# Two PSUM banks for projections and six shared, with new step delays and a new first stage, in a two-layer decoder trunk

## The chip, the core and the metric

The kernel runs on one core of one Trainium2 chip. The core has five engines with a queue of instructions each: TensorE (PE, matrix products), VectorE (DVE), ScalarE (ACT), GpSimd (POOL) and SyncE (SP, which here only issues DMA transfers). Each engine runs its queue in order; engines wait for one another through semaphores. The metric is the device time of one execution in microseconds (us).

## The reference

Everything is float32: 1024 tokens of width 1024, and two layers. Cut to what matters, one layer is:

```python
shift, scale, gate = split(silu(c) @ W_mod + b_mod)
h = rms_norm(x, gain_pre) * (1 + scale) + shift
p = h @ W_in                      # 1024 x 3088, split in three head groups
A = sliding_window_attention(...) # 8 heads, 2 kv heads, window 128
B = retention(...)                # 4 heads, chunks of 128
C = gated_linear_attention(...)   # "GLA": 4 heads, key width 32, chunks of 64
y = concat(A, B, C, each times silu(its gate path)) @ W_out
x = x + gate * rms_norm(y, gain_post)
```

B and C are normalised per head first, and C's decay is computed from the data.

## The kernel before

**Numbers in halves.** Each float32 matrix is split into a high and a low part of a shorter type. A product of two such matrices takes three passes (high by high, high by low, low by high). `project`, `project_T`, `project_2`, `accum` and `prod` emit them: mostly 24 matmuls of 128x512 for one tile of 128 tokens, into one PSUM bank. `mult` (L170) and `transp` (L185) emit every matmul and every transpose, so nearly all PE rows of the profile carry one of these two lines; the tile names tell them apart. `mm` stands for a bank of a projection or an output product, `aux` for a bank of everything else (transposes, scores, states), `arena` for weights.

**Weights.** A weight arrives by DMA in a stage tile `st` (five of these in use), is converted to its high part (ACT L154 or DVE L156, `arena<-st`) and its low part (DVE or POOL L504). These conversions stand in the same in-order queues as all other work of ACT, DVE and POOL, so one that waits for its DMA holds up what is queued behind it.

**PSUM.** There are eight banks of 128x512 float32. `mm()` rotates over `MMB` = 3 of them, `aux()` over the other five. A matmul into a bank waits until the readers of that bank's last content (the "eviction") are done.

**Order on PE.** The program keeps a clock `clk` of its own, to which each matmul adds its length. Work is cut into jobs, generators that emit some instructions and then `yield lat(key, l)`: a delay, after which the job may go on. The delay is a value of the table `L` for the key (a second one for layer 2, `key@1`), plus what the table `X` has for this very occurrence (`"gc2#7"` is the seventh call with key `gc2`). `pump()`, called between matmuls, resumes the jobs whose time has come. So these numbers decide between which matmuls of a projection a small step lands, and nothing else does on PE. Other engines are ordered by the framework's scheduler, which follows from it.

The jobs that matter below: `glaout` ends with two transposes into an `aux` bank, which ACT (L154) and DVE (L1115) then empty. `attnkv` transposes a key tile into an `aux` bank (ACT L988, DVE L989). `glacore` (key names `gc1` to `gc6`) works on a pair of tokens' tiles `p`: two transposes, and then for each of two halves 56 matmuls of 32 rows into four `aux` banks at once, which ACT L1269 and DVE L1270 empty (a "score burst").

**The first stage** (up to 46.6 us) has its order written out by hand: `ORDER_0` for the DMA issues (x0 to x3 parts of the input, w0 to w7 the eight 1 MB parts of `W_mod`, g a part of the first weights), `ORDER_1` for the steps. There S0 to S7 are the products with w0 to w7, C and L take up their results, M and N make the scaled halves of the input, P and Q the first projection's sums, T and U transposes of the input; z and y are fillers, matmuls of a constant whose result is not used. `GLO` says who makes the low halves of two of the first weights.

Of the kernel before, what the change touches and what calls it, by code (L numbers as in the profile page):

```python
# [26 lines left out]
AQ, AK, AV, AG = 0, 512, 640, 768  # L27
# [64 lines left out]
def trunk(ctx: ExitStack, tc: tile.TileContext, ins, cst, out):  # L92
# [40 lines left out]
    def aux(dt=F32):  # L133
        return ps.tile([P, 512], dt, tag="aux", name=nm("aux"), bufs=8 - MMB)

# [579 lines left out]
    def first_stage():  # L715
# [59 lines left out]
        pc = mm()  # L775
# [599 lines left out]
    def y_half(l, t, nh, mixt, ss, yg):  # L1375
        pm = mm()
        w0, w1 = used(l, f"o{2 * nh}"), used(l, f"o{2 * nh + 1}")
        accum(pm.rearrange("p (s n) -> p s n", s=2),
              lambda a, k: mixt[:, a, k, :], lambda b, k: both(w0[:, b, k, 0:256], w1[:, b, k, 0:256]))
        A.activation(yg, pm, AF.Square, accum_out=ss[:, nh:nh + 1])  # L1380
        V.tensor_tensor(yg, pm, modg[l][:, 512 * nh:512 * nh + 512], ALU.mult)

    def y_last(l, mixt, ss, yg):
        s3 = small(3)
        for u in range(2):
            pm = mm()[:, 0:256]
# [121 lines left out]
    def last_output(l, load_mix):  # L1508
# [24 lines left out]
        for p in range(PLAIN // 2):  # L1533
            x, ss, yg = [], [], []
            for t in (2 * p, 2 * p + 1):
                if t + 1 < PLAIN:
                    m[t + 1] = load_mix(l, t + 1)
                x.append(mm())
# [7 lines left out]
            for i, t in enumerate((2 * p, 2 * p + 1)):  # L1546
# [5 lines left out]
                y = mm()  # L1552
# [13 lines left out]
        for p in range(PLAIN // 2, NP_):  # L1566
# [9 lines left out]
            pm = mm()  # L1576
            prod(pm, cur.a[0], "W00")
            s1 = kept(pm)
            pm = mm()
# [4 lines left out]
            pm = mm()  # L1584
# [9 lines left out]
            pm = mm()  # L1594
# [5 lines left out]
            pm = mm()  # L1600
# [3 lines left out]
            if nxt:  # L1604
                nxt.late()
                pump()
                pm = mm()
                prod(pm, a22, "T4")
                summed(yg[o][0], pm, s1, ss[o][:, 0:1], 0)
                job(finish(l, o, ss[o][:, 0:2], yg[o]))  # L1610
                pump()
                continue
# [4 lines left out]
            pm = mm()  # L1617
# [3 lines left out]
            pm = mm()  # L1621
# [10 lines left out]
    def layer(l):  # L1632
# [3 lines left out]
        def do_gates(name, p):  # L1636
            w = used(l, name)
            for t in (2 * p, 2 * p + 1):
                pg = mm()
# [195 lines left out]
ORDER_0 = "g x1 x0 w0 g w1 x2 w2 g w3 w4 x3 w5 w6"  # L1835
ORDER_1 = (
# [4 lines left out]
)  # L1841
GLO = {'AG': (2, 3), 'AV': (1, 0, 2)}
B2, B1, BS, BST, MMB, SMB, BMOD = 10, 8, 11, 5, 3, 3, 3
# [39 lines left out]
}  # L1883
L = {"fx": 0.0, "fx@1": 3.19, "tt6": 10.91, "sw1": 2.36, "ld1": 1.66, "ld2": 1.76, "ld1@1": 0, "ld2@1": 0, "swW00": 5.37, "swT1": 0.43, "swW11": 1.72, "swW10": 6.42, "tt1": 15.2, "tt2": 5.14, "tt3": 7.18, "tt4": 1.84, "rq1": 17.87, "pf3@2": 0.45, "pf3@3": 0.47, "pf4@2": 4.68, "pf4@3": 9.7, "pf5": 0, "mod1": 12.02, "mod2": 2.2, "mod3": 8.51, "mod4": 8.65, "mod5": 4.17, "mod6": 9.91, "pre1": 11.53, "kv1": 4.21, "kv2": 9.26, "aq1": 6.02, "aq7": 6.16, "ag1": 4.54, "aq2": 2.75, "aq6": 6.87, "aq3": 11.06, "aq4": 6.77, "aq5": 4.05, "hn1": 8.92, "hn2": 7.95, "gz1": 18.33, "gz2": 13.43, "gl1": 9.02, "gd3": 17.03, "gc1": 0.98, "gc2": 6.16, "gc3": 1.97, "gc4": 0.1, "gc6": 0.8, "gc5": 1.4, "rc1": 3.56, "rc2": 2.88, "rc3": 7.08, "rc4": 5.77, "fin1": 8.81, "lay1": 0.0, "gc4@1": 0, "mod2@1": 3.98, "mod3@1": 12.43, "mod5@1": 4.3, "mod6@1": 5.5, "pre1@1": 7.09, "kv1@1": 5.87, "kv2@1": 2.64, "aq1@1": 4.85, "aq7@1": 5.14, "ag1@1": 2.87, "aq2@1": 1.05, "aq6@1": 6.78, "aq3@1": 8.64, "aq4@1": 5.47, "aq5@1": 5.83, "hn1@1": 8.28, "hn2@1": 1.35, "gz1@1": 15.9, "gz2@1": 11.94, "gl1@1": 3.26, "gd3@1": 15.44, "gc1@1": 0.0, "gc2@1": 2.01, "gc3@1": 0.83, "gc6@1": 1.61, "gc5@1": 0.72, "rc1@1": 4.88, "rc2@1": 2.79, "rc3@1": 5.12, "rc4@1": 1.23, "fin1@1": 6.41, "lay1@1": 12.76, "mod4@1": 5.36, "mod1@1": 6.02}
# [45 lines left out]
```

## Time and profile before

| what | value |
|---|---|
| three runs | 976.16, 977.75 and 978.88 us, median 977.75 |
| the profiled execution | 978.04 us, span of its trace 976.3 us |
| PE busy | 959.7 us, 98% of the span |
| DVE, ACT, POOL busy | 669.2, 411.0, 247.1 us |
| matmuls | 6296 records |
| DMA | 150.23 MB, mean 154 GB/s |

The profiled execution lies 0.3 us above the median. The span is what the trace covers; 1.7 us of the time lie around it. "PE busy" counts overlapping matmuls as one stretch, and a matmul that runs at half clock is as busy as one at full clock, so busy time alone does not show whether PE worked at its speed; the granted clock (PEclk) has to be read beside it.

### The profile page before, as it was taken

To read this page: it belongs to the slowest core of one execution; us is meant where nothing else is said; L and a number is where in the kernel's file an instruction comes from. 1 tells how busy PE (TensorE), PEld (TensorE's weight loads), DVE (VectorE), ACT (ScalarE), POOL (GpSimd) and SP (SyncE) were. 2 spreads that over 40 slices of the span, in tenths; PEclk is the share of its full clock that TensorE was granted. 3 is DMA by queue.
4 is the path that set the end of the run, shared out by engine and by line. 5 is a ranking of instruction groups with operands and counts; after the bars stand their busy time and mean duration, and the time that the engine had idled before them with its cause. 6 is when DMAs were issued, how large, how long until landed. Compare 5 with 4: busy or idle time off the path is not lost.

```text
span 976.3 us, 17846 instructions
## 1 busy us (share of the span) xinstructions
PE 959.7 (98%) x6296; PEld 787.1 (81%) x6296; DVE 669.2 (69%) x1585; ACT 411.0 (42%) x1147; POOL 247.1 (25%) x310
## 2 busy tenths in 40 slices
PE   7999999999999999999999999999999999999996
PEld 6899888888888777778889988888887877777785
DVE  5795857767686967556676454775665478776885
ACT  3775511232333656523455460133333266655331
POOL 1431101412222324501033101122222034545000
PEclk9999999999999999999999999999999899999998
DMA  9765634414154455687454220441215144488883
GB/s 355 273 185 159 214 91 141 141 43 143 41 179 123 132 148 177 203 266 240 166 170 155 90 66 29 130 134 61 77 49 173 38 127 122 134 244 265 275 276 119
DMA packets 107526, 150.23 MB, mean 154 GB/s; under 512 B 11142, under 2 KB 58536, under 8 KB 106412
## 3 DMA queue, kind: packets, MB, share of 16 engines
q1 hardware_dynamic: 96140, 134.75, 43.8%
q10 hardware_dynamic: 11296, 14.34, 4.1%
q8 instruction: 50, 0.82, 0.3%
q14 instruction: 40, 0.33, 0.1%
HBM read 110.25 MB, written 36.70 MB: 151 GB/s over the span
## 4 chain that ended last, share of the span: by engine, by line
PE 65%; DVE 3%; DMA 2%; issue 1%; ACT 1%; POOL 0%; DVEq 0%; POOLq 0%; SPq 0%; ACTq 0%
PE mm L170 50%; PE aux L170 13%; PE aux L185 3%; DMA st<-in_w_last_dram 1%; DMA mixS<-t 1%; POOL arena L534 0%; DVE t L1518 0%; DVE t L1523 0%; ACT st L1522 0%; DVE t L1419 0%; ACT smx L1074 0%; DVE t L1128 0%; DVE smx L1069 0%; DVE st L541 0%; DVE st L569 0%
## 5 line engine op out<-in xcount | busy, mean ns | idle before, releaser
L170 PE MATMUL mm<-arena,arena 128*128 128x512 f32 (+2 forms) x1344 | 296.3, 373 | 0.0
L170 PE MATMUL mm<-arena 128*128 128x512 f32 (+2 forms) x1248 | 276.0, 373 | 0.0
L170 PEld LDWEIGHTS mm<-arena,arena 128*128 128x128 f32 x1344 | 225.4, 191 | 42.0 <-issue 2.8
L170 PEld LDWEIGHTS mm<-arena 128*128 128x128 f32 x1248 | 211.3, 189 | 40.7 <-issue 3.2
L615 POOL TENSOR_TENSOR sm<-sm,mhalf 128x1 f32<-128x1 f32 (+1 forms) x64 | 57.6, 901 | 303.4 <-DVE sm L612 176.3
L170 PE MATMUL mm<-arena,mx 128*128 128x512 f32 (+1 forms) x564 | 130.6, 387 | 0.3 <-ACT kept L1514 0.3
L170 PEld LDWEIGHTS mm<-arena,mx 128*128 128x128 f32 x564 | 101.6, 188 | 24.5 <-issue 1.9
L154 ACT ACTIVATE t<-aux 128x256 f32<-128x256 f32 (+2 forms) x124 | 52.2, 435 | 104.0 <-PE aux L185 75.8
L504 POOL TENSOR_TENSOR arena<-st,arena 128x512 fp32r<-128x512 f32 x31 | 46.4, 1499 | 123.2 <-ACT arena L154 93.6
L154 ACT ACTIVATE arena<-st 128x512 fp32r<-128x512 f32 x94 | 56.4, 629 | 49.5 <-DMA st<-in_w_in_dram 19.0
L504 DVE TENSOR_TENSOR arena<-st,arena 128x512 fp32r<-128x512 f32 x77 | 64.3, 857 | 4.0 <-ACT arena L154 2.5
L1074 ACT ACTIVATE smx<-smx,sm 128x129 f32<-128x129 f32 x128 | 50.0, 395 | 40.0 <-DVE sm L1071 39.4
L1078 POOL TENSOR_TENSOR smx<-smx,sm 128x512 f32<-128x512 f32 x32 | 36.7, 1146 | 109.9 <-DVE sm L1077 91.4
L321 DVE SCALAR_TENSOR_TENSOR acc<-ms,c_act,acc 128x512 f32<-128x512 f32 x60 | 45.6, 761 | 7.0 <-DMA ms<-in_w_mod_dram 6.1
L170 PEld LDWEIGHTS aux<-t,mx 32*128 32x128 f32 (+1 forms) x896 | 43.4, 196 | 7.1 <-issue 3.1
L1122 ACT ACTIVATE t<-aux 128x256 f32<-128x256 f32 x32 | 12.3, 383 | 86.0 <-PE aux L170 74.5
L170 PE MATMUL aux<-t,mx 32*128 32x32 f32 (+1 forms) x896 | 44.5, 281 | 1.5 <-DVE t L1115 1.1
L1419 DVE SCALAR_TENSOR_TENSOR t<-t,sm,t 128x512 f32<-128x512 f32 x32 | 23.3, 749 | 18.4 <-DMA t<-in_x_dram 12.6
L185 PE MATMUL aux<-c_early,t 128*128 128x128 f32 (+1 forms) x186 | 33.8, 277 | 0.0
L1069 DVE COPY_PREDICATED smx<-c_masks,aux 128x256 f32<-128x256 int32 x64 | 25.2, 446 | 12.5 <-ACT smx L154 12.3
L1127 DVE TENSOR_TENSOR t<-aux,sm 128x256 f32<-128x256 f32 x32 | 13.6, 425 | 29.4 <-POOL sm L615 29.4
L170 PEld LDWEIGHTS aux<-kT,mx 64*128 64x128 f32 x384 | 24.6, 185 | 8.8 <-issue 4.9
(266 smaller groups left out, 1449.1 us busy)
## 6 DMA issues: line engine op xcount, KB each, us to landing
st<-in_w_in_dram SPq DMA_DIRECT2D x96, 256.0 KB, 3.6
ms<-in_w_mod_dram SPq DMA_DIRECT2D x64, 256.0 KB, 3.4
mx<-mixS SPq DMA_DIRECT2D x20, 512.0 KB, 7.1
st<-in_w_last_dram SPq DMA_DIRECT2D x36, 256.0 KB, 3.8
wm<-in_w_m_dram SPq DMA_DIRECT2D x8, 1024.0 KB, 18.0
mixS<-t SPq DMA_DIRECT2D x40, 128.0 KB, 2.1
t<-in_x_dram SPq DMA_DIRECT2D x18, 256.0 KB, 5.0
mixS<-t ACTq DMA_DIRECT2D x32, 128.0 KB, 3.3
```

Source lines behind the costliest of these rows:

```text
L154: A.activation(dst, src, AF.Copy)
L170: T.matmul(dst, lhsT, rhs, start=start, stop=stop)
L185: T.transpose(dst, src, idn)
L321: V.scalar_tensor_tensor(acc, wt, c_act[:, k:k + 1], acc, ALU.mult, ALU.add)
L504: e.tensor_tensor(lo, st, f(hi), ALU.subtract)
L615: G.tensor_tensor(r, r, mhalf[:, :w], ALU.pow)
L1069: V.copy_predicated(sv, curmask.unsqueeze(1).to_broadcast((P, 2, P)), pv[:, :, n // P - 1, :])
L1074: A.activation(sm[:, h, :], sm[:, h, :], AF.Exp, bias=mx[:, h:h + 1], accum_out=sums[:, h:h + 1])
L1078: eng("pn").tensor_tensor(sm[:, :, 0:128], sm[:, :, 0:128], rs.unsqueeze(2).to_broadcast((P, 4, P)), ALU.mult)
L1122: A.activation(sq, po, AF.Square)
L1127: V.tensor_tensor(h4(g1), h4(po), r.unsqueeze(2).to_broadcast((P, 4, 64)), ALU.mult)
L1419: V.scalar_tensor_tensor(xt[j], yg[j], r, xt[j], ALU.mult, ALU.add)
```

## The change

1. `MMB` goes from 3 to 2: `mm()` rotates over two banks, `aux()` over six.
2. A new `bank()` takes an `mm` bank twice and then an `aux` bank. The gate projections (`do_gates`) and the products of the output (`y_half`, `y_last`, `last_output`) take their banks from it. All other projections take `mm()`.
3. In the first stage one small bank (`pc`) comes from `aux()`.
4. `L` and `X` have new values: 237 entries of `X` before, 344 after.
5. `ORDER_0`, `ORDER_1` and `GLO` are written anew.

What is computed, and the matmuls of the layers, stay the same.

```diff
+    turn = [0]
+
+    def bank():
+        turn[0] += 1
+        return aux() if turn[0] % 3 == 0 else mm()
...
-        pc = mm()
+        pc = aux()
...
     def y_half(l, t, nh, mixt, ss, yg):
-        pm = mm()
+        pm = bank()
...
         def do_gates(name, p):
             w = used(l, name)
             for t in (2 * p, 2 * p + 1):
-                pg = mm()
+                pg = bank()
...
-ORDER_0 = "g x1 x0 w0 g w1 x2 w2 g w3 w4 x3 w5 w6"
+ORDER_0 = "g x0 x1 w0 w1 x2 w2 g w3 g x3 w4 w5 w6"
 ORDER_1 = (
...
-    "z1 L1 G q2 S2 G z1 T1 t1 C2 M2A P1 S3 L2 y1 z1 r z1 o2 C3 M3A P2 q3 n2 z1 S4 y1 t1 L3 o3 n3 y2 "
-    "P3 C4 M4V L4 U0 N0AAV K0 y1 r S5 z1 T3 P4 C5 M5V S6 L5 y1 t1 U1 P5 t1 N1AAA C6 M6V t1 S7 z1 G U2 "
-    "a N2AAA L6 R Q0 K1 R K2 C7 r t1 U3 M7V N3VVA L7 P6 K3 Q2 t2 R t1 Q1 t1 R t3 P7 Q3 "
...
+    "S4 P3 C4 t1 U0 M4V L4 N0AAA S5 K0 T3 P4 C5 M5V L5 S6 U1 P5 t1 N1AAA C6 S7 M6V t1 r K1 L6 a U2 Q0 "
+    "G C7 N2AAA t1 K2 U3 N3VVA t3 M7V L7 K3 t1 R R Q1 Q2 P6 P7 R t1 R Q3 t2 "
 )
-GLO = {'AG': (2, 3), 'AV': (1, 0, 2)}
-B2, B1, BS, BST, MMB, SMB, BMOD = 10, 8, 11, 5, 3, 3, 3
+GLO = {'AG': (1, 3, 2), 'AV': (2,)}
+B2, B1, BS, BST, MMB, SMB, BMOD = 10, 8, 11, 5, 2, 3, 3
...
-    "gc1#2": 0.8, "gc1#3": -5.47, "gc1#6": -2.13, "gc1#8": 4.1, "gc2#3": -0.28, "gc2#8": 0.51, "gc3#4": 0.13,
...
+    0.27, "fin1#14": 20.64, "fin1#15": 10.24, "fin1#16": -0.99, "fx#3": -10.35, "fx#4": 0.5, "fx#5": -0.91,
```

What the tables do to the order is seen best in the order itself. In the changed kernel helper lines stand six further down (L176 for `mult`, L191 for `transp`, L160 for L154, L994 for L988, L1260 for L1254). A row is one instruction, or several alike in a row ("x8").

The first place is layer 2, GLA pair 3, at 746 to 754 us of the trace, on PE. `mm_1617` and `mm_1634` are projections; `aux_1629` is the transpose of `attnkv` of tile 7, `aux_1630` the two of `glaout` of tile 5, `aux_1635` those of `glacore`, and `aux_1637` to `aux_1640` the score banks. Before:

```order
L170 MATMUL mm_1617_8531<-arena1_454,arena0_71 128x512 x16
L185 MATMUL aux_1629_8587<-c_early_74,t1_1608_8514 128x128
L170 MATMUL mm_1617_8531<-arena1_454,arena0_71 128x512 x4
L185 MATMUL aux_1630_8595<-c_early_74,t1_1605_8489 128x128 x2
L170 MATMUL mm_1634_8609<-arena1_454,arena0_71 128x512 x8
L185 MATMUL aux_1635_8618<-c_early_74,mx_1376_7323 128x128 x2
L170 MATMUL aux_1637_8623<-t2_1626_8574,mx_1376_7323 128x32
```

After, with `glaout` of tile 5 in `aux_1623` and `attnkv` of tile 7 in `aux_1627`:

```order
L191 MATMUL aux_1623_8562<-c_early_74,t1_1605_8493 128x128 x2
L176 MATMUL mm_1616_8531<-arena1_455,arena0_71 128x512 x4
L191 MATMUL aux_1627_8578<-c_early_74,t1_1607_8514 128x128
L176 MATMUL mm_1616_8531<-arena1_455,arena0_71 128x512 x8
L176 MATMUL mm_1634_8613<-arena1_455,arena0_71 128x512 x8
L191 MATMUL aux_1635_8622<-c_early_74,mx_1390_7373 128x128 x2
L176 MATMUL aux_1637_8627<-t2_1630_8590,mx_1390_7373 128x32
```

Between the two transposes of `glaout` and the score burst stood 8 projection matmuls; now 20 stand there.

The second view is ACT's queue at the same place. Before:

```order
L154 ACTIVATE arena1_454<-st_1642_8669 128x512
L154 ACTIVATE arena1_454<-st_1643_8677 128x512
L154 ACTIVATE arena1_454<-st_1644_8681 128x512
L988 ACTIVATE kT_1422_7519<-aux_1629_8587 128x128
L154 ACTIVATE t1_1631_8598<-aux_1630_8595 128x256
L154 ACTIVATE t1_1632_8601<-aux_1630_8595 128x256
L159 DMA mixF_84<-t1_1631_8598 128x256
L159 DMA mixS_83<-t1_1632_8601 128x256
L1254 ACTIVATE t1_1636_8621<-aux_1635_8618 128x256
```

After:

```order
L160 ACTIVATE t1_1624_8565<-aux_1623_8562 128x256
L160 ACTIVATE t1_1625_8568<-aux_1623_8562 128x256
L165 DMA mixF_84<-t1_1624_8565 128x256
L165 DMA mixS_83<-t1_1625_8568 128x256
L994 ACTIVATE kT_1422_7523<-aux_1627_8578 128x128
L160 ACTIVATE arena1_455<-st_1646_8721 128x512
L160 ACTIVATE arena1_455<-st_1647_8729 128x512
L160 ACTIVATE arena1_455<-st_1648_8733 128x512
L1260 ACTIVATE t1_1636_8625<-aux_1635_8622 128x256
```

The three weight conversions stood ahead of the evictions of `attnkv` and `glaout`; now they stand behind them, and directly ahead of the copy of `glacore`'s transposes.

The third place is layer 1, GLA pair 3, at 285 to 292 us, on PE: the end of the first score burst, the two transposes of a `glaout`, projection matmuls, and the start of the second burst. Before:

```order
L170 MATMUL aux_3383<-t_613_3292 128x4x8
L170 MATMUL aux_3384<-t_613_3292 128x4x8
L185 MATMUL aux_3421<-c_early,t_611_3280 128x128 x2
L170 MATMUL mm_3453<-arena_71,arena_454 128x512 x8
L170 MATMUL aux_3466<-t_612_3291,mx_2041 128x32
L170 MATMUL aux_3467<-t_612_3291,mx_2041 128x32
```

After:

```order
L176 MATMUL aux_3391<-t_614_3300 128x4x8
L176 MATMUL aux_3392<-t_614_3300 128x4x8
L191 MATMUL aux_3433<-c_early,t_610_3280 128x128 x2
L176 MATMUL mm_3461<-arena_71,arena_455 128x512 x12
L176 MATMUL aux_3474<-t_613_3299,mx_2045 128x32
L176 MATMUL aux_3475<-t_613_3299,mx_2045 128x32
```

Twelve projection matmuls part the two bursts where eight did.

The fourth is SP's queue in the first stage, from the first part of `W_mod` on (`wm`; `st` is a part of the first weights, `mx` one of the input). Before:

```order
L732 DMA wm<-in_w_m_dram 128x2048
L159 DMA st_112<-in_w_in_dram 128x512
L732 DMA wm<-in_w_m_dram 128x2048
L735 DMA mx_105<-in_x_dram 128x1024
L732 DMA wm<-in_w_m_dram 128x2048
L159 DMA st_117<-in_w_in_dram 128x512
L732 DMA wm<-in_w_m_dram 128x2048 x2
L735 DMA mx_105<-in_x_dram 128x1024
L732 DMA wm<-in_w_m_dram 128x2048 x3
L159 DMA st_171<-in_w_in_dram 128x512
```

After:

```order
L738 DMA wm<-in_w_m_dram 128x2048 x2
L741 DMA mx_105<-in_x_dram 128x1024
L738 DMA wm<-in_w_m_dram 128x2048
L165 DMA st_115<-in_w_in_dram 128x512
L738 DMA wm<-in_w_m_dram 128x2048
L165 DMA st_118<-in_w_in_dram 128x512
L741 DMA mx_105<-in_x_dram 128x1024
L738 DMA wm<-in_w_m_dram 128x2048 x3
L165 DMA st_162<-in_w_in_dram 128x512
L738 DMA wm<-in_w_m_dram 128x2048
L165 DMA st_200<-in_w_in_dram 128x512
```

One more part of the first weights now goes ahead of the last part of `W_mod`.

More of the change, by code (lines that the diff above doesn't have):

```diff
@@ L1385, in y_last @@
         for u in range(2):
-            pm = mm()[:, 0:256]
+            pm = bank()[:, 0:256]
             w = used(l, f"o{2 + u}")
@@ L1537, in last_output @@
                     m[t + 1] = load_mix(l, t + 1)
-                x.append(mm())
+                x.append(bank())
                 ss.append(small(2))
@@ L1551, in last_output @@
                 summed(yg[i][1], z, s1[i], ss[i][:, 1:2], 1)
-                y = mm()
+                y = bank()
                 prod(y, a[1], "W10")
@@ L1575, in last_output @@
                 nxt.parts()
-            pm = mm()
+            pm = bank()
             prod(pm, cur.a[0], "W00")
             s1 = kept(pm)
-            pm = mm()
+            pm = bank()
             prod(pm, cur.a[1], "W10")
@@ L1583, in last_output @@
                 nxt.plain()
-            pm = mm()
+            pm = bank()
             prod(pm, cur.s2, "T2")
@@ L1593, in last_output @@
                 nxt.early()
-            pm = mm()
+            pm = bank()
             prod(pm, cur.s4, "W11")
@@ L1599, in last_output @@
                 pump()
-            pm = mm()
+            pm = bank()
             prod(pm, cur.s3, "T3")
@@ L1606, in last_output @@
                 pump()
-                pm = mm()
+                pm = bank()
                 prod(pm, a22, "T4")
@@ L1616, in last_output @@
             y, s = yg[o][0], ss[o]
-            pm = mm()
+            pm = bank()
             prod(pm[:, h0], a22, "T4", c=h0)
@@ L1620, in last_output @@
             V.tensor_tensor(s[:, 0:1], s[:, 0:1], s[:, 1:2], ALU.add)
-            pm = mm()
+            pm = bank()
             prod(pm[:, h1], a22, "T4", c=h1)
@@ L1846 @@
 X = {
[36 rows of a table removed]
[53 rows of a table added]
 }
-L = {"fx": 0.0, "fx@1": 3.19, "tt6": 10.91, "sw1": 2.36, "ld1": 1.66, "ld2": 1.76, "ld1@1": 0, "ld2@1": 0, "swW00": 5.37, "swT1": 0.43, "swW11": 1.72, "swW10": 6.42, "tt1": 15.2, "tt2": 5.14, "tt3": 7.18, "tt4": 1.84, "rq1": 17.87, "pf3@2": 0.45, "pf3@3": 0.47, "pf4@2": 4.68, "pf4@3": 9.7, "pf5": 0, "mod1": 12.02, "mod2": 2.2, "mod3": 8.51, "mod4": 8.65, "mod5": 4.17, "mod6": 9.91, "pre1": 11.53, "kv1": 4.21, "kv2": 9.26, "aq1": 6.02, "aq7": 6.16, "ag1": 4.54, "aq2": 2.75, "aq6": 6.87, "aq3": 11.06, "aq4": 6.77, "aq5": 4.05, "hn1": 8.92, "hn2": 7.95, "gz1": 18.33, "gz2": 13.43, "gl1": 9.02, "gd3": 17.03, "gc1": 0.98, "gc2": 6.16, "gc3": 1.97, "gc4": 0.1, "gc6": 0.8, "gc5": 1.4, "rc1": 3.56, "rc2": 2.88, "rc3": 7.08, "rc4": 5.77, "fin1": 8.81, "lay1": 0.0, "gc4@1": 0, "mod2@1": 3.98, "mod3@1": 12.43, "mod5@1": 4.3, "mod6@1": 5.5, "pre1@1": 7.09, "kv1@1": 5.87, "kv2@1": 2.64, "aq1@1": 4.85, "aq7@1": 5.14, "ag1@1": 2.87, "aq2@1": 1.05, "aq6@1": 6.78, "aq3@1": 8.64, "aq4@1": 5.47, "aq5@1": 5.83, "hn1@1": 8.28, "hn2@1": 1.35, "gz1@1": 15.9, "gz2@1": 11.94, "gl1@1": 3.26, "gd3@1": 15.44, "gc1@1": 0.0, "gc2@1": 2.01, "gc3@1": 0.83, "gc6@1": 1.61, "gc5@1": 0.72, "rc1@1": 4.88, "rc2@1": 2.79, "rc3@1": 5.12, "rc4@1": 1.23, "fin1@1": 6.41, "lay1@1": 12.76, "mod4@1": 5.36, "mod1@1": 6.02}
@@ new lines @@
+L = {"fx": 0.0, "fx@1": 3.24, "tt6": 12.28, "sw1": 2.01, "ld1": 1.66, "ld2": 1.76, "ld1@1": 0, "ld2@1": 0.07, "swW00": 5.37, "swT1": 0.43, "swW11": 1.72, "swW10": 6.15, "tt1": 15.57, "tt2": 5.14, "tt3": 7.18, "tt4": 3.16, "rq1": 17.87, "pf3@2": 0.68, "pf3@3": 1.67, "pf4@2": 4.07, "pf4@3": 9.27, "pf5": 0, "mod1": 12.02, "mod2": 2.2, "mod3": 8.51, "mod4": 8.54, "mod5": 4.17, "mod6": 9.91, "pre1": 9.84, "kv1": 4.07, "kv2": 9.26, "aq1": 6.02, "aq7": 6.16, "ag1": 4.54, "aq2": 2.75, "aq6": 6.49, "aq3": 11.06, "aq4": 6.85, "aq5": 4.05, "hn1": 8.92, "hn2": 6.14, "gz1": 18.33, "gz2": 11.8, "gl1": 9.81, "gd3": 17.03, "gc1": 0.98, "gc2": 6.16, "gc3": 1.97, "gc4": 0.1, "gc6": 0.8, "gc5": 1.44, "rc1": 3.56, "rc2": 2.88, "rc3": 7.08, "rc4": 5.77, "fin1": 8.69, "lay1": 0.27, "gc4@1": 0, "mod2@1": 4.09, "mod3@1": 12.43, "mod5@1": 4.25, "mod6@1": 5.5, "pre1@1": 7.09, "kv1@1": 5.87, "kv2@1": 2.64, "aq1@1": 4.88, "aq7@1": 5.14, "ag1@1": 2.87, "aq2@1": 1.05, "aq6@1": 6.78, "aq3@1": 8.64, "aq4@1": 5.48, "aq5@1": 5.73, "hn1@1": 8.28, "hn2@1": 0.73, "gz1@1": 15.9, "gz2@1": 11.94, "gl1@1": 3.31, "gd3@1": 16.2, "gc1@1": 0.0, "gc2@1": 2.01, "gc3@1": 0.83, "gc6@1": 1.61, "gc5@1": 0.72, "rc1@1": 4.88, "rc2@1": 2.79, "rc3@1": 5.12, "rc4@1": 0.8, "fin1@1": 8.37, "lay1@1": 11.61, "mod4@1": 5.36, "mod1@1": 6.02}
```

90 rows, old and new, of tables (ORDER_1, X) are left out of this document.

## Prediction

> **What bounds the kernel now.** I read the page of the profile first, then the windows, then the chain of waits around the places where the windows show a loss. From the page:
>
> ```profile
> PEclk9999999999999999999999999999999899999998
> ...
> PE 65%; DVE 3%; DMA 2%; issue 1%; ACT 1%; POOL 0%; DVEq 0%; POOLq 0%; SPq 0%; ACTq 0%
> ...
> L170 PE MATMUL mm<-arena,arena 128*128 128x512 f32 (+2 forms) x1344 | 296.3, 373 | 0.0
> L170 PE MATMUL mm<-arena 128*128 128x512 f32 (+2 forms) x1248 | 276.0, 373 | 0.0
> ```
>
> PE's matmuls lead the chain that ended last, and the two largest groups are projections and output products into `mm` banks, with nothing waited for ahead of them. The clock dips in two places. Nothing of PE's work in the layers is removed, so the change can gain or lose in three ways only: PE stands, PE runs at a lower clock, or the first stage ends at another time. The windows show where (columns: stretch, length, busy time of PE, PEld, DVE, ACT, POOL, then PEclk):
>
> ```profile
> 250.00:300.00 50.00, 49.66 (x462) 41.40 (x462) 36.92 (x108) 15.93 (x49) 11.77 (x18) 0.97 0.45 136
> 300.00:740.00 440.00, 439.40 (x2833) 362.92 (x2832) 287.31 (x701) 187.11 (x542) 108.33 (x138) 1.00 0.42 132
> 750.00:800.00 50.00, 48.88 (x329) 39.49 (x329) 29.23 (x62) 19.03 (x61) 8.84 (x9) 0.86 0.30 85
> ```
>
> From 300 to 740 PE is idle for 0.6 us and has the full clock. The losses are at 250 to 300 and at 750 to 800. Finer:
>
> ```profile
> 288.04:291.46 3.42, 3.40 (x62) 2.84 (x61) 3.38 (x10) 1.51 (x4) 0.00 (x0) 1.00 0.91 279
> 291.46:294.87 3.41, 3.41 (x10) 2.74 (x10) 2.48 (x7) 0.81 (x4) 0.00 (x0) 0.50 0.57 163
> ...
> 748.84:752.26 3.42, 2.30 (x47) 1.88 (x45) 1.82 (x4) 1.47 (x5) 1.27 (x1) 1.00 0.88 268
> 752.26:755.67 3.41, 3.41 (x28) 2.96 (x25) 0.89 (x4) 0.68 (x4) 0.00 (x0) 0.50 0.75 259
> ...
> 762.50:765.91 3.41, 3.41 (x12) 2.85 (x12) 1.29 (x2) 0.00 (x0) 0.00 (x0) 0.50 0.00 0
> ```
>
> Half clock is granted in one stretch of 3.41 us at 291, and in four together (13.65 us) from 752. Both follow a GLA pair 3 in which PE waited. The chain there (start, length, what):
>
> ```profile
> 285.06 1.75 PE aux L170 x56
> ...
> 287.18 1.84 PE mm L170 x8
> ...
> 289.04 2.34 PE aux L170 x56
> 291.38 0.52 PE aux L185 x2
> 291.90 4.19 PE mm L170 x12
> ...
> 749.62 0.68 DVE t L1019
> ...
> 751.28 2.33 PE aux L170 x50
> 753.62 3.71 PE mm L170 x8
> 757.33 3.14 PE aux L170 x56
> 760.47 3.71 PE mm L170 x8
> 764.18 2.42 PE aux L170 x18
> ```
>
> The first two rows give the sound prices: 1.75 us for a score burst, 1.84 for 8 projection matmuls (0.23 each). At 289.04 the burst takes 2.34; the wait is 0.59. At 749.62 PE has issued 6 of the 56 and stands until 751.28. Why, the rows of ACT and DVE tell:
>
> ```profile
> 748.58 0.63 ACT L154 ACTIVATE arena<-st 128x512 fp32r<-128x512 f32 x1 [2.72 <-DMA st<-in_w_in_dram]
> 749.12 0.26 ACT L988 ACTIVATE kT<-aux 128x128 fp32r<-128x128 f32 x1
> 749.27 0.65 ACT L154 ACTIVATE t<-aux 128x256 f32<-128x256 f32 x2
> ...
> 749.41 0.29 DVE L989 TENSOR_TENSOR kT<-aux,kT 128x128 fp32r<-128x128 f32 x1 [2.59 <-ACT kT L988]
> ...
> 750.81 0.42 DVE L1115 TENSOR_TENSOR t<-aux,t 128x256 fp32r<-128x256 f32 x1
> ```
>
> ACT stood 2.72 us for a weight's DMA. Behind that conversion were queued the copies of `attnkv` and `glaout`, behind these DVE's L989, L1019, L1020 and L1115, and L1115 empties the bank that the fourth score matmul needs. PE's row of the waits names only the last link.
>
> **The change, part by part.** *GLA pair 3 of layer 2.* From 749.62 to 753.62 the burst takes 4.00 us for 1.75, a loss of 2.25, wait and the begin of half clock together. After it come 3.71 for 1.84 (1.87), 3.14 for 1.75 (1.39), 3.71 again (1.87), and from 764.18 to 765.91 half of 1.73 (0.87): 8.25 us in all, about 1.6 of it waiting, the rest clock. The new order puts the copies of `attnkv` and `glaout` ahead of the three conversions on ACT, and 20 projection matmuls (4.6 us) between `glaout`'s transposes and the burst where 8 stood. The eviction by itself is 0.65 on ACT and 0.42 on DVE, so the wait goes. Next in the queue stands `glacore`'s copy (L1254), now behind the conversions. If the weight lands as before, ACT reaches it at 749.2, about when the transposes that it copies are done; hidden, with under 1 us to spare.
>
> *GLA pair 3 of layer 1.* The second burst waits for DVE's L1270 on the first burst's banks. 12 matmuls part the bursts instead of 8, 0.92 us more, against a wait of 0.59; and with six `aux` banks only three of its four banks come from the first burst. The wait goes. The clock's share is 0.15 (0.52 for the 0.37 of two transposes at full clock) and 1.43 (4.19 for 12 times 0.23). Sum 2.17 us.
>
> *Other waits.* The view of PE's waits after 60 us:
>
> ```profile
> PE aux L170 <- DVE t L1115: 1.1, 1, 1.1
> ...
> PE aux L170 <- DVE t L1127: 0.3, 1, 0.3
> ```
>
> The second (at 262.5, GLA pair 2 of layer 1) goes, as with six banks its burst takes the bank of an earlier `glaout`: 0.3. The short waits in the retention and in the output products keep their order; nothing for them.
>
> *Does the clock follow the wait?* The trace grants by stretches of 3.41 us. Bursts alone did not cost it: at 706 to 711 two bursts stand closer together, at full clock (the chain again):
>
> ```profile
> 706.48 1.69 PE aux L170 x56
> 708.18 1.13 PE mm L170 x4
> 709.31 1.72 PE aux L170 x56
> ```
>
> The two bursts with a wait of 0.59 us and more were followed by half clock; the one at 262.5, with 0.3, was not. Once at half clock, the next burst (757.33) takes so long itself that the low clock is kept until 765.91. I take both losses as gone. [...]
>
> *Two banks for the projections.* A bank is wanted again after one other projection, 24 times 0.23 = 5.6 us. A `project_T` bank has two DVE readers of 0.68 (rows of L1019, L1020), so about 4.2 us are left for whatever stands ahead of them on DVE. Below, this costs nothing; above, with ACT or DVE held 2.7 us as at 748 and a table load besides, a wait of about 1 us at two or three places. Banks taken by `bank()` rotate over three as before. With the moves of some hundred steps by tables, some new small waits are sure; between 0 and 3 us I take 0.8, nearer the lower end, since 440 us of the old order hold only 0.6.
>
> *First stage.* PE works from 26.34 on without a gap but 0.22:
>
> ```profile
> 23.20:33.62 10.42, 10.42 (x116) 8.15 (x113) 6.31 (x19) 4.55 (x11) 1.98 (x4) 1.00 1.02 410
> 26.34:46.62 20.28, 20.06 (x193) 17.27 (x193) 16.29 (x36) 14.41 (x28) 8.95 (x8) 1.00 0.78 287
> ...
> 36.04 1.07 PE L170 MATMUL aux<-wm,c_act 128*32 128x256 f32 x16
> 37.04 0.49 PE L170 MATMUL aux<-c_early 128*128 128x128 f32 x2
> 37.37 0.60 PE L185 MATMUL mm<-c_early,mx 128*128 128x128 f32 x4
> ```
>
> The row at 37.04 is a filler, 0.33 us from start to start. Seven stand after S4, at 0.33 at most 2.3 us, and somewhat less where three follow one another; I take 2.0. The new order has none after S4, so PE alone would end that much earlier. Against that, one more part of 256 KB goes ahead of w7, at 410 GB/s 0.64 us. w7 was issued at 15.6 and took 18.0:
>
> ```profile
> L732 SPq DMA_DIRECT2D wm<-in_w_m_dram x8: 327/328/431, 3.3 to 15.6; - x8
> ...
> DMA to landing us min/median/max: 18.0/18.0/18.0
> ```
>
> so it would land at 34.2. S7, at 36.04 with six of the fillers ahead (some 1.7 us), would come at 34.3: just met. DVE's scaling (16.29 busy of 20.28) may bind then. The fillers added ahead of S0 stand where PE waits for w0 anyway; `GLO` gives POOL another low half, and POOL is busy for 8.95 of the 20.28, so that is hidden (if POOL came late, the first projections would wait for it); `pc` in `aux` takes a bank that no score needs yet. These three at nothing. From a gain of 2.0 to a loss of 0.6, I take 1.5 gained.
>
> *Sum* against the profiled execution of 978.04: 8.25 + 2.17 + 0.3 + 1.5 - 0.8 = 11.4, so 966.6 us; that execution lies 0.3 above the median of 977.75.
>
> **The rivals.** *Half clock stays or comes back.* The cause would be the bursts' own small matmuls and where the 3.41 us stretches fall, and the waits only a companion (the burst of 757 alone kept the clock low). Against it: of the sixteen bursts thirteen had no half clock in or behind them. It would also come so at pair 3 of layer 2 if the weights land more than 1 us later than 748.58, since ACT would then be late for `glacore`'s copies. Only the waits of 1.6 + 0.59 + 0.3, the first stage and the 0.8 count: 974.9; if only the short drop stays, 968.2.
>
> *The orders cost what they save.* The waits move one bank on, the first stage is bound by w7: 976 to 980.
>
> *Slower: the projections wait for their two banks.* The two groups of the page hold 1344 + 1248 matmuls, 108 projections and products of 24. Each takes a bank that was free early before, when three rotated. If eviction delays often pass the 4.2 us, in the stretches where DVE and ACT convert weights, PE waits at the start of many of them: 0.15 us on the mean is 16.2 us, and the time 966.6 - 0.8 + 16.2 = 982.0. It decides from a mean of 0.11 on (12.2 us of gain over 108). For it speaks that DVE is busy 287 of the 440 us from 300 to 740; against it that PE waits for nothing there with three banks, and that one 5.6 us projection covers the rest.
>
> **How the numbers follow.** Forecast 0.50 (963 to 970); half clock stays 0.26 (970 to 976); no change 0.12; slower 0.12. The range reaches from 962.5, where no new wait appears and the fillers are gained in full, to 977.5, through the second case and the first part of the third. 0.3% (2.9 us) is about what a measurement can tell from no change: faster by more takes the first two cases, 0.76; within it 0.12; slower 0.12.
>
> **What the profile would show.** PEclk 1.00 at 250 to 300 and 750 to 800; bursts of pair 3 at 1.7 us; L1115 gone from the waits; ACT's copies of `glaout` ahead of the conversion; the first 256-wide projection at about 45 instead of 46.62. I am wrong if a half-clock stretch remains beside any GLA pair, if PE waits at starts of projections for the eviction of an `mm` bank, or if S7 waits for its DMA.

## The result and the profile after

The changed kernel takes 966.42 us (median of 6 runs, 965.55 to 969.06) against 976.18 us for the kernel before (6 runs, 972.71 to 978.88): a ratio of 0.9908, 95% interval 0.9883 to 0.9932. The profiled execution took 967.82 us, 1.4 above the median, with a span of 966.1. Forecast were 966.6 us.

The page, then the windows (columns as in the prediction; the number behind POOL's busy time is PEclk) and the chain at the two places where the prediction put the gain:

```profile
PEclk9999999999999999999999999999999999999999
...
PE 90%; DMA 4%; DVE 3%; issue 1%; POOL 1%; ACT 1%; SPq 0%; DVEq 0%; POOLq 0%; ACTq 0%
```

```profile
250.00:300.00 50.00, 50.00 (x483) 41.92 (x481) 39.06 (x117) 17.04 (x52) 12.48 (x19) 1.00 0.45 138
...
735.00:770.00 35.00, 35.00 (x278) 28.94 (x277) 23.06 (x57) 12.86 (x38) 6.86 (x6) 1.00 0.45 134
```

```profile
285.33 1.69 PE aux L176 x56
287.02 0.37 PE aux L191 x2
287.39 2.76 PE mm L176 x12
290.16 1.69 PE aux L176 x56
...
746.68 1.69 PE aux L176 x56
748.38 2.06 PE mm L176 x8
750.43 1.69 PE aux L176 x56
```

All four bursts take 1.69 us, where 1.75, 2.34, 4.00 and 3.14 stood, and PE has the full clock around them. In the kernel before, the second window read:

```profile
735.00:770.00 35.00, 33.88 (x244) 28.04 (x243) 17.32 (x49) 8.86 (x27) 6.95 (x6) 0.80 0.35 110
```

The order that the prediction rested on is seen on ACT and DVE:

```profile
741.95 0.66 ACT L160 ACTIVATE t<-aux 128x256 f32<-128x256 f32 x2
...
744.63 0.28 ACT L994 ACTIVATE kT<-aux 128x128 fp32r<-128x128 f32 x1 [2.03 <-PE mm L176]
744.81 1.66 ACT L160 ACTIVATE arena<-st 128x512 fp32r<-128x512 f32 x3
...
742.92 0.41 DVE L1121 TENSOR_TENSOR t<-aux,t 128x256 fp32r<-128x256 f32 x1
```

`glaout`'s bank is empty at 743.33, 3.4 us ahead of the burst, and the three conversions find their weights there. What PE still waits for, from 40 us on:

```profile
PE aux L176 <- DVE arena L835: 2.2, 1, 2.2
PE mm L176 <- ACT kept L1520: 0.9, 1, 0.9
```

The first of these is new, and in the first stage. To see where time came and went, I matched the two traces by counting PE's matmuls that read weights (3456 in each, counted from 0). Number 240 begins at 69.55 us before and 1.25 later after; number 900 (244.56) 0.93 later; 1080 (313.39) 1.97 earlier; 2700 (738.40) 2.95 earlier; 2760 (766.53) 10.89 earlier; the trace ends 10.23 earlier. So the first stage lost 1.25, layer 1's GLA gained 2.9, layer 2's GLA pair 3 gained 7.9, the stretches between gained about 1.3 in sum, and the wait for `kept` gave 0.65 back.

### The profile page after: what moved, and what is told of

It reads as the page before. It is cut to its first block, busy times and chain, and to the rows that moved or that the text cites. A ratio compares the mean times of both kernels' runs of the same rounds, so it can differ in the third digit from the quotient of the medians.

```text
span 966.1 us, 17877 instructions
## 1 busy us (share of the span) xinstructions
PE 949.9 (98%) x6304; PEld 780.8 (81%) x6304; DVE 670.2 (69%) x1585; ACT 411.8 (43%) x1148; POOL 238.9 (25%) x309
## 4 chain that ended last, share of the span: by engine, by line
PE 90%; DMA 4%; DVE 3%; issue 1%; POOL 1%; ACT 1%; SPq 0%; DVEq 0%; POOLq 0%; ACTq 0%
PE mm L176 61%; PE aux L176 25%; PE aux L191 4%; DMA wm<-in_w_m_dram 2%; DMA st<-in_w_last_dram 1%; DMA t<-aoS 1%; POOL arena L540 0%; DVE t L1524 0%; DVE t L1529 0%; ACT st L1528 0%; DMA c_early<-cst_early_dram 0%; DVE t L1425 0%; DVE sincos L398 0%; PE mm L191 0%; DVE t L1758 0%
## 5 line engine op out<-in xcount | busy, mean ns | idle before, releaser
L176 PE MATMUL mm<-arena,arena 128*128 128x512 f32 (+2 forms) x1200 | 273.9, 379 | 0.0
L176 PE MATMUL mm<-arena 128*128 128x512 f32 (+2 forms) x1152 | 263.3, 381 | 0.0
L176 PEld LDWEIGHTS mm<-arena,arena 128*128 128x128 f32 x1200 | 205.1, 189 | 41.4 <-issue 2.9
L176 PEld LDWEIGHTS mm<-arena 128*128 128x128 f32 x1152 | 199.8, 189 | 40.5 <-issue 2.7
L160 ACT ACTIVATE t<-aux 128x256 f32<-128x256 f32 (+2 forms) x124 | 51.9, 434 | 96.8 <-PE aux L191 73.2
L176 PE MATMUL mm<-arena,mx 128*128 128x512 f32 (+1 forms) x396 | 91.0, 384 | 0.9 <-ACT kept L1520 0.9
L176 PEld LDWEIGHTS mm<-arena,mx 128*128 128x128 f32 x396 | 70.4, 188 | 17.8 <-issue 1.9
L160 ACT ACTIVATE arena<-st 128x512 fp32r<-128x512 f32 x94 | 56.0, 626 | 40.0 <-PE mm L176 14.7
L176 PE MATMUL aux<-arena,mx 128*128 128x512 f32 x252 | 61.1, 397 | 0.0
L176 PEld LDWEIGHTS aux<-arena,mx 128*128 128x128 f32 x252 | 47.2, 188 | 11.4 <-issue 0.4
L176 PEld LDWEIGHTS aux<-t,mx 32*128 32x128 f32 (+1 forms) x896 | 39.7, 187 | 5.1 <-issue 2.3
L176 PE MATMUL aux<-t,mx 32*128 32x32 f32 (+1 forms) x896 | 40.7, 272 | 0.0
```

The source lines that it names most:

```text
L160: A.activation(dst, src, AF.Copy)
L176: T.matmul(dst, lhsT, rhs, start=start, stop=stop)
```

## The experiments

Two questions were open. Which part removed the losses at the GLA pairs, the order of the steps or the sixth bank? And why did the first stage lose where a gain of 1.5 was forecast? All times below are medians. They come from three comparisons, each on one chip and beside the kernel before, whose own medians there were 973.2 to 974.4 us.

**The banks alone, and the delays alone.** The bank change with the old tables:

```diff
 # the kernel before
+    def bank():                      # as in the change, with all its uses; also pc from aux()
+        turn[0] += 1
+        return aux() if turn[0] % 3 == 0 else mm()
-B2, B1, BS, BST, MMB, SMB, BMOD = 10, 8, 11, 5, 3, 3, 3
+B2, B1, BS, BST, MMB, SMB, BMOD = 10, 8, 11, 5, 2, 3, 3
```

> The kernel before with the bank change alone (two mm banks, six aux, bank()), and the old delays and first stage. Theory 1 (the order of the steps removed the losses, as predicted): the stall at GLA pair 3 of layer 2 stays, 974 to 976 us. Theory 2 (one more aux bank is enough: the fourth score bank is then the one that attnkv's transpose had, which DVE empties at 749.7, not glaout's, emptied at 751.2): the wait and the half clock go, as do those of layer 1, about 966 us. Rival (two banks make projections wait): over 978 us, with waits for evictions of mm banks in the waits.

Measured: 969.98 us, ratio 0.9952 (0.9926 to 0.9979). The window of pair 3, and PE's waits:

```profile
735.00:770.00 35.00, 35.00 (x288) 28.96 (x287) 22.73 (x61) 12.37 (x34) 7.57 (x6) 1.00 0.43 127
```

```profile
PE mm L176 <- DVE t L1147: 1.1, 1, 1.1
```

Theory 2 holds for this place: with six banks PE does not stand there, and the order is the old one. The burst's fourth bank is then another. The time is 4 us above the 966 that theory 2 gave. The price of two banks shows once, 1.1 us at a gate projection of layer 2 (L1147 is L1141 of the old numbering). In another kernel below (`gc3#7` changed), with three banks, L1141 holds PE for 1.0 us in two waits at the same place, so even this one is not the two banks' alone.

The other half is the changed kernel with the old split of the banks:

```diff
 # the changed kernel
-        return aux() if turn[0] % 3 == 0 else mm()
+        return mm()
-        pc = aux()
+        pc = mm()
-B2, B1, BS, BST, MMB, SMB, BMOD = 10, 8, 11, 5, 2, 3, 3
+B2, B1, BS, BST, MMB, SMB, BMOD = 10, 8, 11, 5, 3, 3, 3
```

> The changed kernel with three mm banks and five aux as before, all new delays and orders kept. Theory (the new delays alone keep glaout's and attnkv's evictions ahead of the bursts): 966 to 967.5 us as the changed kernel, perhaps 0.3 more at GLA pair 2 of layer 1. Rival (the delays need the sixth aux bank): a wait at GLA pairs 2 or 3 comes back, with half clock behind it, 969 to 976 us.

Measured: 968.72 us, ratio 0.9946 (0.9926 to 0.9966). Its windows at 262 us and at pair 3 of layer 2:

```profile
262.00:272.00 10.00, 9.52 (x131) 8.02 (x129) 9.44 (x27) 4.91 (x18) 4.00 (x6) 0.87 0.41 115
...
735.00:770.00 35.00, 35.00 (x289) 28.99 (x288) 23.32 (x62) 12.18 (x35) 7.86 (x7) 1.00 0.41 120
```

At pair 3 the order alone is enough too. At pair 2 of layer 1 the wait came back (0.48 us idle) with half clock behind it, as the rival had it for that place. Each half of the change thus removes the large loss by itself; the sixth bank is needed only at the small one. By the medians neither half alone reaches the time of both together (966.89 us in the same comparison, with the old first stage, below); only part of the difference was traced.

**One delay.** The order at pair 3 in one number, added to the kernel before, and taken out of the changed one:

```diff
 # the kernel before
-... "hn1#29": -0.1, "hn1#32": -2.03, ...
+... "hn1#29": -0.1, "hn1#30": -2.8, "hn1#32": -2.03, ...
```

> The kernel before with one entry added to X: hn1#30 = -2.8 (the delay ahead of the last two transposes of glaout, tile 5 of layer 2), so that they stand 20 projection matmuls ahead of the burst instead of 8, and ACT copies them ahead of the second and third weight conversion. Five aux banks as before. Theory (the eviction's place in the queues makes the 8.25 us): wait and half clock at 749 to 766 go, 8 us gained, about 968 us, the 2.2 us at 289 stay. Rival (the clock falls there by the bursts alone): the wait of 1.6 goes and half clock stays, about 974.5.

Measured: 969.75 us, ratio 0.996 (0.9931 to 0.9989).

```profile
289.21 1.86 PE L170 MATMUL aux<-t,mx 32*128 32x32 f32 x47
...
291.34 0.44 PE L185 MATMUL aux<-c_early,t 128*128 128x128 f32 x2
...
285.00:300.00 15.00, 15.00 (x178) 12.81 (x176) 13.09 (x32) 5.31 (x16) 1.00 (x3) 1.00 0.70 209
735.00:770.00 35.00, 35.00 (x285) 28.85 (x285) 22.72 (x59) 12.12 (x35) 7.44 (x6) 1.00 0.41 125
```

The last row is pair 3 of layer 2: the wait and half clock are gone, by one number of the table. The rows above are from layer 1, where nothing was changed, and were a surprise. The second burst there takes 2.13 us from 289.21 to 291.34, so its wait is there (1.69 without), but no half clock follows. The wait and the clock are not tied as firmly as the prediction had it.

```diff
 # the changed kernel
-... "hn1#30": -2.8, ...
+... "hn1#30": 0.0, ...
```

> The changed kernel with hn1#30 put to 0, so that ACT copies glaout's transposes behind all three weight conversions again, with 8 projection matmuls between them and the burst. Six aux banks. Theory 1 (the order alone removed the stall): it comes back, with half clock, 974 to 976 us. Theory 2 (six banks are enough by themselves, since the burst's first half no longer takes glaout's bank): no more than 0.5 us of change, 966 to 967.5 us.

Measured: 965.25 us, ratio 0.99 (0.9854 to 0.9945), and at pair 3:

```profile
735.00:770.00 35.00, 34.98 (x277) 28.68 (x276) 22.69 (x57) 13.59 (x41) 6.90 (x7) 1.00 0.45 138
```

Theory 2 again: with six banks the order of `glaout` does not matter at this place.

**Is it the wait that costs the clock?** The second burst of layer 1 put further from the first:

```diff
 # the kernel before
-... "gc3#7": 0.16, ...
+... "gc3#7": 1.1, ...
```

> The kernel before with gc3#7 at 1.1 instead of 0.16: at GLA pair 3 of layer 1, 12 projection matmuls stand between the two bursts instead of 8. Theory (the wait of 0.59 us makes the short stretch of half clock): both go, 2.2 us gained behind 291 us, about 974 to 975.5 us, the loss at 750 stays. Rival (half clock at 291 comes from where the stretches fall): 0.6 gained at most, or the half clock moves.

Measured: 972.94 us, ratio 0.9992 (0.9965 to 1.0018): no difference that can be told. Its windows:

```profile
285.00:300.00 15.00, 14.89 (x174) 11.77 (x172) 11.96 (x29) 5.08 (x16) 0.14 (x1) 1.00 0.67 196
735.00:770.00 35.00, 33.88 (x264) 27.78 (x263) 20.60 (x57) 10.98 (x30) 7.59 (x7) 0.95 0.39 118
```

This miss taught more than a hit. At 285 to 300 there is no half clock, but neither is there in the kernel above, which left this place alone; the edit proves nothing about the clock there. And at pair 3 of layer 2, with the wait as before (1.12 us idle), the mean clock over 35 us is 0.95 and not 0.80: one stretch of half clock, not four. So the wait of layer 1 was followed by one stretch in one trace and by none in another, and the wait of layer 2 by four and by one.

The wait was then kept and PE given work in it:

```diff
 # the kernel before, in glacore, ahead of the score matmul
+                    if (l, p, c, s, h) == (1, 3, 0, 1, 3):
+                        for _ in range(6):
+                            mult(sp[0][:, 2 * P:3 * P], ident, ident, True, True, 0.0)
```

> The kernel before with six matmuls of 128x128 of a constant (results unused) put ahead of the fourth score matmul of GLA pair 3 in layer 2, where PE stands waiting. The wait for the bank stays, PE works in it. Theory (half clock follows low work in a stretch of 3.41 us): the wait keeps its 1.6 us, half clock from 752 to 766 goes, 6.5 us gained, about 969.5 us. Rival (half clock comes from the bursts alone, or from something that PE's filling does not change): 976 to 978 us.

Measured: 971.2 us, ratio 0.9965 (0.9942 to 0.9987). PE's timeline, then DVE's L1115, then the window:

```profile
747.91 0.42 PE L170 MATMUL aux<-t,mx 32*128 32x32 f32 x6
748.26 1.60 PE L170 MATMUL aux<-c_early 128*128 128x128 f32 x12
749.79 1.41 PE L170 MATMUL aux<-t,mx 32*128 32x32 f32 x41
...
748.96 0.41 DVE L1115 TENSOR_TENSOR t<-aux,t 128x256 fp32r<-128x256 f32 x1
...
735.00:770.00 35.00, 35.00 (x291) 29.08 (x290) 20.89 (x56) 11.64 (x32) 7.57 (x6) 1.00 0.40 115
```

DVE frees the bank at 749.37, as late in the pair as before (749.60 would be the same, since PE is 1.63 us ahead here), and the clock stays at full. By counted matmuls the pair is 6.1 us shorter than in the kernel before, with the wait still paid (the filling overshot it by 0.42). This fits the theory. Since the unfilled wait of this place was followed by one stretch of half clock in one trace and by four in another, one trace would not prove it; the medians, 971.2 against 974.4, agree.

**The first stage.** The changed kernel with `ORDER_0`, `ORDER_1` and `GLO` of before:

```diff
 # the changed kernel
-ORDER_0 = "g x0 x1 w0 w1 x2 w2 g w3 g x3 w4 w5 w6"
+ORDER_0 = "g x1 x0 w0 g w1 x2 w2 g w3 w4 x3 w5 w6"
...
-GLO = {'AG': (1, 3, 2), 'AV': (2,)}
+GLO = {'AG': (2, 3), 'AV': (1, 0, 2)}
```

> The changed kernel with ORDER_0, ORDER_1 and GLO of before. Theory (the new first stage is a loss of 1.25 us, by a wait of 2.2 us for DVE and a stretch of half clock at 45 to 48.5 us): both are gone, the 256-wide first projections start at about 46.6, and the time is 1.0 to 1.5 us under the changed kernel's (about 965 us median), with the rest of the trace as in the changed kernel. Rival (the first stage as predicted saves, and 1.25 us are lost by other means before 52 us, such as the rotation of two banks): the loss stays or grows, 967 to 970 us.

Measured: 966.89 us, ratio 0.9934 (0.9906 to 0.9961), no gain over the changed kernel's 0.9908. Its 256-wide projections begin at 47.80; the same order began them at 46.62 in the kernel before:

```profile
47.80 5.92 PE L176 MATMUL mm<-arena,arena 128*128 128x256 f32 x48
```

So the first stage moves by a microsecond from one execution to the next with its order unchanged (here it is late from the first sums on), and the 1.25 us of one pair of traces are no measure of the new order. That theory falls in its size. By counted matmuls at number 240, the six traces with the old order (its own among them) lie from 0.41 ahead of the kernel before to 1.16 behind it, the four with the new order and the wait unfilled from 0.36 ahead to 1.25 behind: no gain, and no clear loss. The wait for L835 is real all the same. In the changed kernel, DVE, POOL and PE:

```profile
41.48 1.91 DVE L398 TENSOR_SCALAR sincos<-sincos 128x512 f32<-128x512 f32 x1
43.31 0.53 DVE L829 TENSOR_SCALAR t<-mm,mod,mod 128x256 f32<-128x256 f32 x1
43.87 1.14 DVE L835 CAST arena<-t 128x256 fp32r<-128x256 f32 x1
...
41.30 1.81 POOL L939 MEMSET mx<- 128x2048 f32 x1 [0.28 <-DMA c_late<-cst_late_dram]
...
45.06 4.05 PE L176 MATMUL aux<-arena 128*128 128x272 f32 x18 [2.18 <-DVE arena L835]
48.95 5.91 PE L176 MATMUL mm<-arena,arena 128*128 128x256 f32 x48
```

L829 scales the last block of the input (M7V); L835 makes the high half that PE wants. Ahead of them stands the sine table (t3), with L398 at its end, drawn out to 1.91 us. One step was moved:

```diff
 # the changed kernel, ORDER_1
-... K2 U3 N3VVA t3 M7V L7 K3 t1 R R ...
+... K2 U3 N3VVA M7V L7 K3 t3 t1 R R ...
```

> The changed kernel with one step of ORDER_1 moved: t3 (three steps of the sine table: an ACT table load, two ACT and two DVE instructions) goes from ahead of M7V to behind K3. Theory (these steps hold DVE and ACT while the last block of the input waits to be scaled): DVE scales block 7 at about 40.7 instead of 43.3 us, PE's 2.2 us wait and the half clock behind it go, 2.2 to 3.9 us are gained, about 963 to 964 us median. Rival (PE waits for what POOL and DVE hold each other up with, wherever the table steps stand; or the table is then late for its first use): no gain, 966 to 968 us.

Measured: 962.94 us, ratio 0.9881 (0.9848 to 0.9915). DVE and PE:

```profile
38.55 1.44 DVE L829 TENSOR_SCALAR t<-mm,mod,mod 128x256 f32<-128x256 f32 x3
40.03 0.45 DVE L835 CAST arena<-t 128x256 fp32r<-128x256 f32 x1
...
42.18 0.43 DVE L398 TENSOR_SCALAR sincos<-sincos 128x512 f32<-128x512 f32 x1
...
44.09 5.92 PE L176 MATMUL mm<-arena,arena 128*128 128x256 f32 x48
```

PE waits for nothing there, and the projections begin at 44.09, where the prediction had put the gain (about 45). The same kernel was then run beside the changed kernel itself, and beside one in which y8, a filler of PE's, is put into the wait:

```diff
 # the changed kernel, ORDER_1
-... Q1 Q2 P6 P7 R t1 R Q3 t2
+... Q1 Q2 P6 y8 P7 R t1 R Q3 t2
```

> The changed kernel with eight matmuls of 128x128 of a constant (results unused) between P6 and P7 of the first stage, where PE waits 2.2 us for DVE's L835. The wait stays, PE works in it. Theory (half clock at 45 to 48.5 follows the low work of the stretch before): the wait's end stays at 45.0, half clock behind it goes, 1.5 to 1.7 us under the changed kernel on the same chip. Rival (the clock does not follow what PE does in the wait): no difference, or up to 0.3 us slower.

> The changed kernel once more, for a comparison on the same chip: 965.5 to 967.5 us median, with the wait of 2.2 us for L835 and half clock behind it.

> The changed kernel with the step t3 behind K3 once more, beside the changed kernel itself on the same chip. If the gain is the first stage's, 3.3 to 4.2 us under it (about 962.5 to 963.5), of which the filled wait gets 1.5 to 1.7 and the shorter wait the rest; if it was another chip's, under 1 us.

Measured on one chip: 966.28 us with the wait filled (ratio 0.9915, 0.9885 to 0.9945), 965.63 for the changed kernel (0.9911, 0.9876 to 0.9945), 963.35 with the table behind (0.9882, 0.9844 to 0.9919). The table's place is worth 2.3 us by these medians (five of its six executions lie below all six of the changed kernel's), less than the 3.3 to 4.2 expected; filling the wait is worth nothing that can be told, where 1.5 to 1.7 were expected.

Half clock was expected behind the wait of the changed kernel here, and did not come, though PE is idle for 2.18 us as in the first trace. What differs is where the stretches of 3.41 us lie. In each trace all changes of the clock are whole multiples of 3.413 us apart (82 and 135 of them between the three drops at 11.57, 291.46 and 752.26 us in the kernel before), and from one trace to the next the grid is shifted. On its grid the first trace of the changed kernel reads so around the wait, then the one here:

```profile
42.09:45.50 3.41, 1.23 (x10) 1.02 (x9) 3.34 (x5) 1.75 (x4) 2.77 (x3) 1.00 0.11 36
45.50:48.92 3.42, 3.42 (x17) 3.42 (x16) 2.82 (x5) 1.92 (x4) 1.75 (x4) 0.50 0.03 8
...
40.09:43.50 3.41, 2.50 (x21) 2.28 (x19) 3.10 (x4) 3.41 (x7) 3.13 (x4) 1.00 0.50 183
43.50:46.91 3.41, 2.14 (x17) 2.14 (x18) 3.34 (x6) 1.18 (x3) 1.89 (x3) 1.00 0.06 17
46.91:50.33 3.42, 3.42 (x31) 3.42 (x30) 2.22 (x7) 3.41 (x14) 1.79 (x9) 1.00 0.19 62
```

There the whole wait fell into one stretch, which left PE 1.23 us of work, and the next ran at half clock. Here it was split over two, with 2.50 and 2.14 us of work, and none did.

With the wait filled, the projections begin at 46.29, but PE then waits elsewhere:

```profile
54.09 1.09 PE L191 MATMUL aux<-c_early,xl 128*128 128x128 f32 x8 [0.95 <-DVE xl L679]
```

What PE gains ahead of DVE it gives back 8 us later. By counted matmuls both stand 0.3 us ahead of the kernel before at 70 us, the table behind 2.56 (3.13 in its first trace). The version with the table behind beats both kernels: 962.94 and 963.35 in two comparisons.

## Why the prediction was right, and where not

The time (966.42 for 966.6) is closer than its terms: the sum was made for the profiled execution, which took 967.82, 1.2 more; that the median met it within 0.2 is luck. Term by term, between the two profiled executions:

- GLA pair 3 of layer 2: 8.25 forecast, 7.9 measured. Right in size for that trace. The cause was told too narrowly: "the wait goes" by the new order is true, but the sixth bank alone does it too, and the prediction gave the bank no part there. Either edit was enough.
- GLA pair 3 of layer 1 with pair 2: 2.17 and 0.3 forecast, 2.9 measured. At pair 2 the sixth bank is what counts: with five, 0.48 us of waiting came back.
- *First stage*, 1.5 us gained: this step failed. PE alone did run ahead, by 1.2 us at 38 us. Then it stood 2.18 us, and the 256-wide projections began at 48.95 where about 45 was forecast. The sentence that DVE's scaling "may bind then" was the outcome; it was left in the 0.5 taken off the 2.0, and it took the whole gain: the step t3 stands ahead of M7V. POOL was put at nothing, and two of DVE's steps took 1.48 and 0.69 us longer beside its work than in the kernel with the table moved (last section). The term about w7 was harmless: S7 began at 35.16 with no wait. Read properly, the order of ORDER_1 showed t3 there.
- *New small waits*, 0.8 against: 0.65 came at one place, the product that waits for ACT's `kept`. It was 0.3 before, 0.9 here, and 2.0 in the second trace of the version with the table behind, where a stretch of half clock followed at 902.84 (ten matmuls from 902.27 took 4.14 us, twelve ahead of them 2.97):

```profile
PE mm L176 <- ACT kept L1520: 2.0, 1, 2.0
```

  Why it varies so was not settled. About 1.3 us were gained in the stretches between, which the sum did not have; 0.6 of them are PE's idle time from 313 to 738 us of the kernel before.
- *Does the clock follow the wait?* The prediction took both losses as gone because the waits go, and this held in the changed kernel's trace. Its rule ("a burst with a wait of 0.59 us and more") does not hold as it stands: the wait of layer 1 was followed by one stretch of half clock or none, that of layer 2 by four or one, and the 2.18 us of the first stage by one or none. What the traces show in its place is the work that falls into one stretch of the grid. I weighted the time of each matmul by the share of 128 rows that its weights take (a score matmul of 32 rows counts a quarter) and summed it by stretch, from 14 to 950 us of all thirteen traces. The eight stretches at full clock that were followed by half clock hold 0.68 to 1.69 us of such work; every other one, about 3500, holds 1.77 or more. So by this count a burst of 1.69 us weighs little, a short wait beside it (0.59 us at 289.04 in the kernel before) was enough where both fell into one stretch, and filling the wait (2.17 in its stretch) kept the clock. This is a count made after the fact, over these kernels alone; no run was made to test it elsewhere.
- The profiled execution was not a typical one. Over 58 executions of the kernel before, timed on three chips beside the experiments, the time ran from 969.0 to 979.7 us, and went with the mean granted clock (correlation -0.87; 0.987 at 978.2, 0.998 at 969.4). The one with the trace lay near the slow end. A sum made against it, 978.04 less 11.4, met the changed kernel, it seems, because the losses that vary are the ones that went (its own twelve executions reach only from 965.2 to 969.1). The same 11.4 off the median of 974.0 in the last comparison would have been 3 us too low (962.6 against 965.63).
- The rivals. Half clock stayed beside no GLA pair in either trace of the changed kernel; it came once in the first stage. "The orders cost what they save" came in the first stage only, by DVE and not by w7. That two banks make projections wait stayed small: one wait of 1.1 us in the bank change alone. But the wait for `kept` is, as far as the rows tell, of that kind too, since `kept` is ACT's copy out of an `mm` bank: 0.9 in the changed kernel, against 0.3 with three banks before and 0.6 with three banks and the new tables.

## What to carry over

Follow a wait past its last link: the bank's release named a DVE copy, but what held it was a weight conversion in ACT's queue, which stood 2.72 us for a DMA, and either a changed queue order or one more bank removed it. In these traces half clock came behind stretches with little work (0.68 to 1.69 us by the count above), their grid was shifted from one trace to the next (42.09 and 40.09 us in the two of the changed kernel), and the time of the kernel before ran from 969.0 to 979.7 us: find the grid in each trace before a window is read, and set a loss read from one trace beside the spread of the times and their clocks. And when the busiest engine's filler is taken out, look at once who is next: here a table computed ahead of the scaling (L398 took 1.91 us beside POOL's memset, 0.43 where the table was moved) took the whole gain, and moving that one step gave 2.3 us.

## What the runs showed of the hardware

Two of DVE's instructions took longer when POOL worked beside them. L398 took 1.91 us at 41.48, ending 0.28 after POOL's memset of 41.30 to 43.11; the same instruction took 0.43 in the kernel with the table moved. L835 took 1.14 at 43.87, ending 0.15 after a conversion on POOL (43.60 to 44.86), and 0.45 in the other kernel. Not every instruction did: L396 took 0.69 in both kernels, in the latter wholly beside such a memset. What makes one instruction grow and another not, no run shows. The two instructions grew by 1.48 and 0.69 us, 2.17 together, about as much as PE's wait of 2.18. So POOL's work may account for most of that wait, and not the table's own length; no run moved POOL's work and left the table.

That a wait of 2.18 us passed without half clock where it was split over two stretches of 3.41 us (2.50 and 2.14 us of work in them), and one of 0.59 beside a burst of small matmuls (1.69 us of weighted work in its stretch) was followed by it, was not expected either.
